# A two-stream transformer kernel on one core: three durations and the pace in its emission clock are changed

## The chip, the cores and the metric

One Trainium2 chip, of which the kernel uses one core. The metric is the device time of one execution, in microseconds (us): the median of several runs. The core has TensorE (PE; its weight loads are shown apart, as PEld), VectorE (DVE), ScalarE (ACT), GpSimd (POOL) and SyncE (SP), which issues the loads from DRAM.

## What is computed

Two blocks, one after the other, on 256 tokens of 1024 features, batch 1. The first block has four layers: short convolution, a state-space mixer (SSM), RWKV-7, short convolution; each is followed by a gated projection and a layer norm. Its output is the x of the second block, which has two layers and a second stream, the context (256 more positions, `ctx`), that doesn't depend on the first block at all before the attention:

```python
def reference(x, ..., c_2, ctx_2, c_ctx_2, ...):
    x = first_block(x, p, conv_w_in, ..., ln_g, ln_b)
    return second_block(x, c_2, ctx_2, c_ctx_2, ...)

def _rwkv_step(state, inp):            # 256 steps, 16 heads of 64
    r_t, w_t, k_t, v_t, kk_t, a_t = inp
    sa = jnp.einsum("bhvk,bhk->bhv", state, -kk_t)
    state = (state * w_t[:, :, None, :] + sa[..., None] * (kk_t * a_t)[:, :, None, :]
             + v_t[..., None] * k_t[:, :, None, :])
    return state, jnp.einsum("bhvk,bhk->bhv", state, r_t)

def second_block(x, c, ctx, ...):
    for l in range(2):
        mod_x = split(silu(c) @ ada_w[l] + ada_b[l])       # the modulation, 9 parts; mod_c alike
        x   = half_ffn(x, ...);   ctx = half_ffn(ctx, ...)     # swiglu, 2816 wide
        y_x, y_c = mixer_ab(hx, hc, ...) if l == 0 else mixer_cd(hx, hc, ...)
        x = half_ffn(x + mod_x[5] * y_x, ...)
        if l == 0: ctx = half_ffn(ctx + mod_c[5] * y_c, ...)
    return x
```

Mixer AB is two sorts of attention whose queries and keys are rms-normed head by head (and rotated, for the tokens); mixer CD is a gated linear recurrence beside a neighbourhood attention.

## The kernel before

Activations lie feature-major: 128 features on the partitions, 256 tokens in the free dimension. A weight is loaded from DRAM as fp32 blocks of 128 x 1024 (`Net.get`, queue SP) and split into two fp32r parts, `whi` by an ACT copy (L599) and `wlo` by a DVE subtraction (L600); a product of it is three fp32r products of 256 columns per chunk of 128 features (`mm3`: hi x hi, hi x lo, lo x hi). The work within the mixers (RWKV heads, SSM, attention) is in fp32 products, of 64, 128 or 256 columns.

Each engine executes its instructions in the order in which it was given them. That order comes from the emission. A generator (`Stream`) emits the instructions of one stream: X is the first block and then the tokens of the second, C is the context. `weave` runs from a clock, `Net.now() = cost + idle`: `cost` is the sum of the durations that `TensorE.matmul` puts on products, `idle` the time in which it believes that TensorE has to wait. Each generator yields where TensorE needs what other engines must first deliver, and is `ready` again at a time that a model of ACT and DVE gives (`Engine.place`: a fixed part and the free size by a rate, in the first gap that is long enough). The first stream in the list that is ready goes on, so C's products fall where the clock sees X waiting. `par` does the same within a stream among two or three chains, such as the heads of RWKV (`heads`, three at a time) or the rms norms of AB (`key` and `head_tile`, two at a time); in the heads, other streams' products go in pieces of 4 chunks, 12 products (`mm3g`, `PIECE`). The third stream, the modulation (`ada`), is emitted by pace: one block each `GAPS` us of the clock, by stage.

During the heads (L1153 and after), C is in its first feed-forward network, whose first half's products are `ps_mm<-h_hi,whi`, `ps_mm<-h_lo,whi` and `ps_mm<-h_hi,wlo`. The recurrence of a pair of heads in chunks of 64 steps goes on in the banks `ps_ca`, `ps_cb` and `ps_mm` with `sv`, `rw_a` and `rw_b`; between its steps ACT and DVE copy from the banks.

`rsqrt` (L677) takes Ln and Exp of the same tile (`tc`) by ACT, then a Newton step by DVE. `act` keeps note of the ACT table set it believes to be there, and issues a load of the set that holds both functions (L393) when Ln comes and the note says another; loads of line 402 are put in when the program is built, ahead of an activation whose function isn't in the set that is there.

A second listing of the names: `x`, `ctx` residual streams; `tc`, `ta`, `tb`, `td` temporaries; `ps_*` PSUM banks; `cs_*` constants; `qb`, `kb` queries and keys of AB.

Of the kernel before, what the change touches and what calls it, by code (L numbers as in the profile page):

```python
# [19 lines left out]
S = 256  # L20
NCH = D // 128
ALPHA = 8 ** 0.25
# [3 lines left out]
# order of emission  # L26
EARLY = 40  # how far back work that nothing waits for may fill an engine's gaps
FINE = 3  # products in pieces in the SSM core (1) and the RWKV heads (2)
PIECE = 4  # K chunks in such a piece
PARTS = 3  # parts of layer 0's modulation that come first  # L30
GAPS = (6.5, 10., 12., 12.)  # the modulation's pace
SLACK = 2  # how far behind VectorE may be for the modulation to go on ...
LATE = 60  # ... unless it is this late
# [3 lines left out]
# ---------------------------------------------------------------- host layout  # L37
def tiles_of(w, cols):
    """[K, M] -> the K x 128 column tiles starting at each entry of cols, as [n, K, 128]."""
    return np.stack([w[:, c:c + 128] for c in cols])  # L40


def blocks(tl, mt=1):
    """[n, K, 128] column tiles -> [n / mt, 128, K / 128 * mt * 128] blocks, K-chunk major."""
# [10 lines left out]
def wsplit(w):  # L55
    """Blocks of 256 columns by half of the K chunks: [M / 256 * 2, 128, 4 * 256]"""
# [5 lines left out]
def fcols(v):  # L62
    """[..., F] -> [128, prod(...) * F / 128]: a feature's value on its partition."""
    v = np.asarray(v)
    return v.reshape(-1, v.shape[-1] // 128, 128).transpose(2, 0, 1).reshape(128, -1)


def tok(x):
    """[T, F] -> [128, F / 128, T]"""
# [17 lines left out]
def constants():  # L87
# [10 lines left out]
    # RWKV chunks of 64 steps: rows beta_s | k_s, columns alpha_t | r_t  # L98
# [35 lines left out]
def rope_head(dim):  # L134
    """cos, sin [S, dim] of the axial rotation, and the [dim, dim] matrix M with rotated = u @ M."""
# [20 lines left out]
def pack(inp):  # L156
    """The input arrays in the layouts that the program loads; no arithmetic."""
# [13 lines left out]
    # SSM: partition (e, p), column pair: group 2 * pair + e, state p  # L171
# [16 lines left out]
    # RWKV  # L188
# [12 lines left out]
    # second block  # L201
# [13 lines left out]
    # heads of A: tile j holds heads j and j + 4, which use the two key heads  # L215
# [21 lines left out]
    # relative position bias spread over query and key positions; positions outside the window hold -1e30  # L237
# [8 lines left out]
    # gains, which the program scales  # L246
# [13 lines left out]
# ---------------------------------------------------------------- the program  # L260
# [1686 lines left out]
```

## Time and profile before

| | |
|---|---|
| three runs | 2931.11, 2926.54, 2930.72 us; median 2930.72 |
| profiled execution | span 2931.2 us; its own time is not listed apart from the runs |
| PE, PEld, DVE, ACT busy | 96%, 90%, 73%, 56% of the span |
| DMA | 454.89 MB, mean 155 GB/s |
| mean granted TensorE clock | 0.985 of full speed |

The profile names groups by line, engine and tile. An fp32 product shows as two records, an fp32r product of 256 columns as one. Records of products overlap, since products are pipelined; the time from one to the next is their pitch. In the order of the work, the first block fills the first 1060 us or so (the heads are at 545 to 785 us), then comes the second block's tokens beside what is left of the context (the tokens' AB projection is at 1535 to 1690 us, their AB attention follows).

### The profile page before, as it was taken

The numbers are of one execution on the slowest core, as the hardware profiler recorded it, in microseconds if no ns is written. First come the engines' busy times: TensorE is split into PE (matmuls) and PEld (weight loads), VectorE is DVE, ScalarE is ACT, GpSimd is POOL, SyncE is SP. The second block draws the span as 40 slices with busy tenths as digits, with TensorE's granted clock in tenths as the row PEclk, the third lists the DMA queues.
The fourth block names the chain that finished last, engine by engine and source line by source line (L and its number), as shares of the span: only waits on it lengthen the run. The fifth ranks groups of instructions, "written<-read, shape, count | busy, mean of one in ns | idle before, by whom it ended". The sixth has DMA issues, their size and how long they took to land.

```text
span 2931.2 us, 58792 instructions
## 1 busy us (share of the span) xinstructions
PE 2814.3 (96%) x23798; PEld 2652.5 (90%) x23798; DVE 2142.3 (73%) x4116; ACT 1631.4 (56%) x3069; POOL 16.6 (1%) x42
## 2 busy tenths in 40 slices
PE   8989998899999999999999999999999999999999
PEld 8977788787999999998999978999999999996999
DVE  8876777666678788898898887877855336676655
ACT  5644556766646464778566766544522224466443
POOL 0000000000000000000000000000000000000000
PEclk9989998999999999999999999999999999999999
DMA  7632353200466666666675644666544323221554
GB/s 266 216 130 94 100 185 123 81 23 33 140 213 203 215 201 221 205 194 190 196 224 182 194 155 129 208 223 212 181 144 125 100 82 102 92 87 57 160 182 142
DMA packets 129296, 454.89 MB, mean 155 GB/s; under 512 B 14336, under 2 KB 18688, under 8 KB 128384
## 3 DMA queue, kind: packets, MB, share of 16 engines
q1 hardware_dynamic: 129024, 451.13, 48.3%
q8 instruction: 187, 3.06, 0.4%
q14 instruction: 85, 0.70, 0.1%
HBM read 450.02 MB, written 1.05 MB: 154 GB/s over the span
## 4 chain that ended last, share of the span: by engine, by line
PE 68%; DVE 14%; DMA 8%; ACT 6%; issue 4%; SPq 0%; DVEq 0%; ACTq 0%
PE ps_mm L431 56%; DMA w<-in_ada_dram 7%; PE ps_ca L431 5%; PE ps_cb L431 5%; DVE wlo L600 5%; DVE junk L1354 3%; ACT whi L599 2%; DVE tc L402 1%; PE ps_st L431 1%; PE ps_cb L435 1%; ACT L402 1%; ACT rw_b L402 1%; ACT tc L402 1%; DVE h_lo L402 1%; DMA w<-in_ffn_in_dram 1%
## 5 line engine op out<-in xcount | busy, mean ns | idle before, releaser
L599 ACT ACTIVATE whi<-w 128x1024 fp32r<-128x1024 f32 (+1 forms) x687 | 715.9, 1044 | 731.1 <-PE ps_mm L431 474.1
L600 DVE TENSOR_TENSOR wlo<-w,whi 128x1024 fp32r<-128x1024 f32 (+1 forms) x687 | 826.3, 1204 | 240.7 <-ACT whi L599 238.8
L431 PE MATMUL ps_mm<-h_hi,whi 128*128 128x256 f32 x3024 | 868.0, 289 | 6.1 <-ACT h_hi L402 4.4
L431 PE MATMUL ps_mm<-h_lo,whi 128*128 128x256 f32 x3024 | 856.0, 284 | 2.5 <-DVE h_lo L402 2.4
L431 PE MATMUL ps_mm<-h_hi,wlo 128*128 128x256 f32 x3024 | 853.2, 283 | 3.1 <-DVE wlo L600 3.0
L431 PEld LDWEIGHTS ps_mm<-h_hi,whi 128*128 128x128 f32 x3024 | 569.7, 189 | 15.8 <-ACT h_hi L402 6.3
L431 PEld LDWEIGHTS ps_mm<-h_lo,whi 128*128 128x128 f32 x3024 | 570.2, 189 | 8.7 <-DVE h_lo L402 3.7
L431 PEld LDWEIGHTS ps_mm<-h_hi,wlo 128*128 128x128 f32 x3024 | 570.9, 189 | 7.4 <-DVE wlo L600 4.9
L1354 DVE SCALAR_TENSOR_TENSOR junk<-w,cond 128x1024 bf16<-128x1024 f32 x288 | 351.9, 1222 | 125.9 <-DMA w<-in_ada_dram 124.8
L431 PE MATMUL ps_mm<-d_hi,whi 128*128 128x256 f32 x1232 | 353.4, 287 | 0.9 <-DVE ctx L402 0.4
L431 PE MATMUL ps_mm<-d_hi,wlo 128*128 128x256 f32 x1232 | 348.5, 283 | 3.6 <-DVE wlo L600 3.6
L431 PE MATMUL ps_mm<-d_lo,whi 128*128 128x256 f32 x1232 | 349.6, 284 | 0.0
L431 PEld LDWEIGHTS ps_mm<-d_hi,wlo 128*128 128x128 f32 x1232 | 233.2, 189 | 4.9 <-DVE wlo L600 4.7
L431 PEld LDWEIGHTS ps_mm<-d_hi,whi 128*128 128x128 f32 x1232 | 232.4, 189 | 4.0 <-issue 2.6
L431 PEld LDWEIGHTS ps_mm<-d_lo,whi 128*128 128x128 f32 x1232 | 232.4, 189 | 2.7 <-issue 1.6
L402 DVE TENSOR_TENSOR td<-td,ps_mm 128x256 f32<-128x256 f32 x154 | 64.5, 419 | 82.3 <-PE ps_mm L431 78.8
L402 ACT ACTIVATE d_hi<-td 128x256 fp32r<-128x256 f32 x154 | 63.0, 409 | 79.2 <-DVE td L402 78.4
L402 ACT ACT_TABLE_LOAD x81 | 103.9, 1283 | 2.5 <-PEq L1938 0.7
L431 PE MATMUL ps_mm<-x_hi,whi 128*128 128x256 f32 x256 | 73.6, 287 | 12.4 <-ACT whi L599 12.4
L402 ACT ACTIVATE tc<-tc 128x256 f32<-128x256 f32 x182 | 75.2, 413 | 6.0 <-DVE tc L402 3.1
L402 ACT ACTIVATE td<-ps_mm 128x256 f32<-128x256 f32 x154 | 57.1, 373 | 33.5 <-PE ps_mm L431 33.1
L431 PE MATMUL ps_mm<-xs_hi,whi 128*128 128x256 f32 x256 | 72.7, 284 | 2.7 <-ACT whi L599 1.6
(459 smaller groups left out, 5466.2 us busy)
## 6 DMA issues: line engine op xcount, KB each, us to landing
w<-in_ffn_in_dram SPq DMA_DIRECT2D x268, 512.0 KB, 4.0
w<-in_ada_dram SPq DMA_DIRECT2D x144, 512.0 KB, 4.3
w<-in_ffn_out_dram SPq DMA_DIRECT2D x96, 512.0 KB, 4.1
w<-in_conv_in_dram SPq DMA_DIRECT2D x64, 512.0 KB, 4.5
w<-in_ffn_out_dram SPq DMA_DIRECT2D x48, 384.0 KB, 3.5
w<-in_ab_in_dram SPq DMA_DIRECT2D x34, 512.0 KB, 4.4
w<-in_ple_gate_dram SPq DMA_DIRECT2D x32, 512.0 KB, 4.4
w<-in_conv_out_dram SPq DMA_DIRECT2D x16, 512.0 KB, 4.6
```

Source lines behind the costliest of these rows:

```text
L402: return f(**kw)
L431: self.t.matmul(out, lhsT=lhsT, rhs=rhs, start=start, stop=stop)
L435: self.t.transpose(out, in_, ident)
L599: nc.scalar.activation(out=hi[:, :n], in_=w[:, :n], func=AF.Copy)
L600: nc.vector.tensor_tensor(out=lo[:, :n], in0=w[:, :n], in1=hi[:, :n].bitcast(F32), op=ALU.subtract)
L1354: nc.vector.scalar_tensor_tensor(out=self.junk, in0=w, scalar=1.0, in1=cb[:, s], op0=ALU.mult, op1=ALU.mult, accum_out=m[:, t, s:s + 1])
```

## The change

Four numbers of the emission clock, and what follows from them for the order. An fp32r product is priced 0.011 us longer (256 columns: 0.1087 to 0.1197 us, the constant 0.002 included), an fp32 product with 33 to 64 output rows 0.055 us shorter (64 columns: 0.115 to 0.060 us), a scan on DVE at 1/1.9 of the rate, and the pace of the modulation is stretched from 6.5, 10, 12 and 12 us to 7.2, 11, 13 and 13. No instruction's form or data changes. The rest of the diff takes out comments and docstrings; since the scan's rate adds a line, what stood on L402 and L431 stands on L403 and L432.

```diff
-GAPS = (6.5, 10., 12., 12.)  # the modulation's pace
+GAPS = (7.2, 11., 13., 13.)
...
             ins = [v for k, v in kw.items() if hasattr(v, "tensor") and k not in ("out", "accum_out")]
-            end = self.place(max(m.ready(v, self) for v in ins + outs), self.fixed + free_size(outs[0]) / self.rate)
+            rate = self.rate / 1.9 if name == "tensor_tensor_scan" else self.rate
+            end = self.place(max(m.ready(v, self) for v in ins + outs), self.fixed + free_size(outs[0]) / rate)
...
         if rhs.dtype == F32R:
-            dur = n / 2400.0
+            dur = n / 2400.0 + 0.011
         elif m > 64:
             dur = max(n, 128) / 600.0
         else:
-            dur = 0.06 + max(n, 32) / (1200.0 if m > 32 else 2400.0)
+            dur = 0.005 + max(n, 32) / 1200.0 if m > 32 else 0.06 + max(n, 32) / 2400.0
         self.count(dur + 0.002, out, [lhsT, rhs])
```

As built, the number of PE products is the same; weight blocks loaded and split rise by 4 (blocks that both streams want and that were shared), ACT table loads from 114 to 144.

TensorE in the RWKV heads, where a head (`rw_a_5503`, in bank `ps_cb`) comes to the end of its preparation while the one in `ps_ca` is in its recurrence. `h_hi`, `h_lo` with `whi`, `wlo` are the context's products. Before:

```order
L431 MATMUL ps_cb<-rw_a_5503 128x128 x8
L435 MATMUL ps_cb<-cs_base,rw_a_5503 128x64 x4
L431 MATMUL ps_ca<-sv_4376,rw_b_5501 64x64 x2
L431 MATMUL ps_mm<-rw_b_5507 64x64
L435 MATMUL ps_cb<-cs_base,rw_a_5503 128x64 x4
L431 MATMUL ps_ca<-rw_a_5500,rw_b_5501 64x64 x2
L431 MATMUL ps_cb<-sv_4376,rw_b_5504 64x64 x2
L431 MATMUL ps_mm<-cs_base,rw_b_5507 64x64 x5
L431 MATMUL ps_ca<-sv_4376,rw_b_5501 64x64 x2
L431 MATMUL ps_ca<-rw_b_5501,sv_4376 64x64 x2
L431 MATMUL ps_cb<-rw_a_5503,rw_b_5504 64x64 x2
L431 MATMUL ps_mm<-cs_base,rw_b_5507 64x64 x3
```

And now:

```order
L432 MATMUL ps_cb<-rw_a_5503 128x128 x8
L436 MATMUL ps_cb<-cs_base,rw_a_5503 128x64 x4
L432 MATMUL ps_ca<-sv_4376,rw_b_5501 64x64
L432 MATMUL ps_ca<-rw_a_5500 64x64
L432 MATMUL ps_ca<-sv_4376,rw_b_5501 64x64
L432 MATMUL ps_ca<-rw_a_5500 64x64
L432 MATMUL ps_mm<-h_hi,wlo 128x256
L432 MATMUL ps_mm<-h_hi,whi 128x256
L436 MATMUL ps_cb<-cs_base,rw_a_5503 128x64 x4
L432 MATMUL ps_ca<-rw_a_5500,rw_b_5501 64x64 x2
L432 MATMUL ps_cb<-sv_4376,rw_b_5504 64x64 x2
L432 MATMUL ps_mm<-h_lo,whi 128x256
```

The context's products, of which there was none before among these steps, now stand between the groups of a head's 64-column products.

ScalarE in the tokens' AB projection, where the rms norms of the heads' keys and queries take Ln (`tc<-ps_st,fixed_66`) and Exp with Square (`tc<-tc`) beside the splits of weights (`whi<-w`). Before:

```order
L402 ACTIVATE tc<-ps_st,fixed_66 128x256
L402 ACTIVATE tc<-tc 128x256 x2
L599 ACTIVATE whi<-w 128x1024
L402 ACTIVATE ta<-kb_12361 128x256
L402 ACTIVATE tc<-ps_st,fixed_66 128x256
L402 ACTIVATE tc<-tc 128x256 x2
L402 ACTIVATE ta<-kb_12361 128x256
L599 ACTIVATE whi<-w 128x1024
L402 ACTIVATE tc<-ps_st,fixed_66 128x256
L402 ACTIVATE tc<-tc 128x256 x2
```

And now:

```order
L403 ACT_TABLE_LOAD
L403 ACTIVATE tc<-ps_st,fixed_66 128x256
L600 ACTIVATE whi<-w 128x1024
L403 ACT_TABLE_LOAD
L403 ACTIVATE tc<-tc 128x256
L403 ACTIVATE ta<-kb_12938 128x256
L403 ACTIVATE tc<-tc 128x256
L600 ACTIVATE whi<-w 128x1024 x2
L403 ACT_TABLE_LOAD
L403 ACTIVATE tc<-ps_st,fixed_66 128x256
L403 ACT_TABLE_LOAD
L403 ACTIVATE tc<-tc 128x256 x2
```

Each Ln and each Exp now has a table load ahead of it; before, none stood among them, after one load ahead of the first. Among the 22 loads more in this projection, those of some eight to twelve norms come in such pairs.

## Rows read from the trace of the kernel before

**Rows 1.** The page: span, busy time by engine, shares of the chain that ended last.
```profile
span 2931.2 us, 58792 instructions
...
PE 2814.3 (96%) x23798; PEld 2652.5 (90%) x23798; DVE 2142.3 (73%) x4116; ACT 1631.4 (56%) x3069; POOL 16.6 (1%) x42
...
PE 68%; DVE 14%; DMA 8%; ACT 6%; issue 4%; SPq 0%; DVEq 0%; ACTq 0%
```

**Rows 2.** The chain of waits in order of time: start us, us, what.
```profile
2106.35 339.99 PE ps_mm L431 x2831
```

**Rows 3.** Windows of the heads: stretch, length, busy PE, PEld, DVE, ACT, POOL, clock, DMA share, GB/s.
```profile
545.00:785.00 240.00, 222.86 (x3461) 189.22 (x3462) 148.62 (x362) 160.36 (x424) 0.00 (x0) 0.96 0.16 49
560.00:740.00 180.00, 169.57 (x2933) 143.29 (x2934) 110.24 (x281) 116.35 (x333) 0.00 (x0) 0.98 0.09 30
740.00:780.00 40.00, 40.00 (x433) 35.41 (x430) 20.50 (x37) 26.16 (x56) 0.00 (x0) 1.00 0.43 133
```

**Rows 4.** The same windows, instructions on tile whi alone; no POOL column.
```profile
545.00:785.00 240.00, 52.53 (x260) 40.35 (x260) 19.56 (x16) 17.84 (x17) 0.96 0.16 49
560.00:740.00 180.00, 22.84 (x112) 17.35 (x112) 8.54 (x7) 8.10 (x8) 0.98 0.09 30
740.00:780.00 40.00, 25.66 (x128) 19.85 (x129) 9.80 (x8) 7.78 (x8) 1.00 0.43 133
```

**Rows 5.** The same windows, tile wlo alone; no ACT and POOL columns.
```profile
545.00:785.00 240.00, 37.13 (x129) 24.32 (x130) 19.56 (x16) 0.96 0.16 49
560.00:740.00 180.00, 15.98 (x56) 10.52 (x56) 8.54 (x7) 0.98 0.09 30
740.00:780.00 40.00, 18.22 (x64) 11.99 (x64) 9.80 (x8) 1.00 0.43 133
```

**Rows 6.** Groups by line and form, PE, 545 to 785 us: busy us, mean ns, idle before.
```profile
L431 PE MATMUL ps_st<-rw_b,cs_base 128*128 128x256 f32 x34 | 11.4, 418 | 1.0 <-ACT rw_a L402 0.9
...
L431 PE MATMUL ps_cb<-cs_base,rw_b 128*64 128x64 f32 x192 | 9.9, 227 | 0.0
...
L431 PE MATMUL ps_ca<-rw_a 128*128 128x128 f32 x48 | 6.6, 283 | 0.0
...
L431 PE MATMUL ps_mm<-rw_a 128*128 128x128 f32 x32 | 5.3, 323 | 0.0
...
L431 PE MATMUL ps_mm<-rw_b,cs_base 128*128 128x256 f32 x10 | 3.5, 431 | 0.1
```

**Rows 7.** Timeline of PE in the heads: start us, us, what.
```profile
746.77 0.69 PE L431 MATMUL ps_cb<-cs_base,rw_b 128*64 128x64 f32 x16
```

**Rows 8.** Groups by form, DVE, whole span: the SSM's scan.
```profile
L402 DVE TENSOR_TENSOR_SCAN ssm_s<-rho,ssm_s 128x128 f32<-128x128 f32 x64 | 23.5, 411 | 0.0
```

**Rows 9.** Groups by form, ACT, whole span: table loads.
```profile
L402 ACT ACT_TABLE_LOAD x81 | 103.9, 1283 | 2.5 <-PEq L1938 0.7 <-PE ps_mm L431 0.4
...
L393 ACT ACT_TABLE_LOAD x33 | 42.3, 1283 | 0.6
```

**Rows 10.** Timeline of ACT around one table load.
```profile
1386.46 1.06 ACT L599 ACTIVATE whi<-w 128x1024 fp32r<-128x1024 f32 x1 [1.56 <-issue]
1387.54 1.28 ACT L402 ACT_TABLE_LOAD   x1
1388.83 0.38 ACT L402 ACTIVATE td<-ps_mm 128x256 f32<-128x256 f32 x1
```

**Rows 11.** Windows of AB: projection, two pieces of it, attention; columns as in rows 3.
```profile
1535.00:1690.00 155.00, 148.26 (x1117) 142.01 (x1116) 135.58 (x258) 108.71 (x181) 0.00 (x0) 0.99 0.59 189
...
1640.80:1644.20 3.40, 0.70 (x5) 0.47 (x4) 2.16 (x4) 3.03 (x4) 0.00 (x0) 1.00 0.33 129
1644.20:1647.60 3.40, 3.40 (x18) 3.31 (x17) 3.40 (x8) 0.90 (x1) 0.00 (x0) 0.50 0.45 143
...
1690.00:1830.00 140.00, 138.62 (x956) 110.63 (x956) 111.75 (x238) 90.77 (x166) 0.00 (x0) 1.00 0.45 141
```

**Rows 12.** Waits, 1580 to 1690 us: us in total, times, longest us.
```profile
ACT whi L599 <- PE ps_mm L431: 21.5, 17, 2.8
```

## The prediction

> **What bounds the kernel now.** I read the page first, then the chain of waits, then the stretches one by one. The page puts TensorE at 96% busy and gives PE 68% of the chain that ended last [rows 1]. The chain shows what sort of work this is: one piece of it runs 339.99 us through 2831 products with nothing ahead of it [rows 2]. That is 339.99 / 2831 = 0.120 us for one fp32r product of 256 columns. So an fp32r product that is moved gains 0.120 us if it lands where TensorE would stand idle, and nothing if it lands where TensorE is full. Hence I look for stretches in which TensorE is not full and in which the change alters what stands on its queue. Two matter: the RWKV heads (545 to 785 us) and the tokens' AB projection (1535 to 1690 us).
>
> **How full TensorE is in the heads.** Its busy row says 222.86 of 240 us [rows 3], but matmul records overlap, so I count by pitch. Two pieces of evidence set it. Sixteen records of 64 columns took 0.69 us [rows 7], and one lasts 0.227 us [rows 6]: (0.69 - 0.227) / 15 = 0.031 us from one to the next. Wider fp32 records last 0.283 us (128 columns) and 0.418 us (256) [rows 6]; with the same overlap their pitches are 0.031 + 0.056 = 0.087 and 0.031 + 0.191 = 0.222 us. The context's products here are the 260 on whi and 129 on wlo [rows 4, 5]: 389 x 0.120 = 46.7 us. The other 3461 - 389 = 3072 records [rows 3] are the heads' own: 78 of 256 columns (four groups, of 34, 20, 14 and 10) and 128 of 128 columns (three, of 48, 48 and 32; the first and the last of each stand in [rows 6]) make 17.3 + 11.1 us, the other 2866 x 0.031 make 88.8 us, in all 117.2 (0.038 each on average). Work: 163.9 of 240 us; 76 us, **32%, is lost** to the chain that runs from TensorE to VectorE or ScalarE and back. From 560 to 740 us, where the context has 112 + 56 = 168 products, the same count gives 20.2 + 2765 x 0.038 = 125.3 of 180, 30% lost. From 740 to 780, with 128 + 64 = 192 context products in 40 us, it is 23.0 + 241 x 0.038 = 32.2, 19.5% lost [rows 3 to 5]. More context work, less loss.
>
> **The change, part by part.** No product is added or taken away; the prices only steer the emission.
>
> 1. *Heads.* With 64-column products at 0.06 us and not 0.115 us, the clock no longer credits the heads' products with time that they don't take, and it sees TensorE waiting. By the order, context products among the heads' products go from 480 to 936, and they now stand between the steps of a head's recurrence, where before runs of over 400 products held none. The 456 more (456 x 0.120 = 54.7 us) leave a later place where the context ran densely, at the chain's pitch. The heads' stretch then holds 163.9 + 54.7 = 218.6 us of work. At the loss of 740 to 780 us, the nearest stretch with much context work, it lasts 218.6 / 0.805 = 271.6, 31.6 more; the net is 54.7 - 31.6 = **-23 us**. The bounds: all of it in gaps that exist (-54.7), or a loss that stays at 30% (218.6 / 0.70 = 312, +72, net +18). The value taken is that of the row that is most like what the order shows.
>  With the 19 weight blocks (24 products each) come 19 loads of 512 KB on SP's queue, issued earlier, 19 splits on ScalarE (17.84 / 17 = 1.05 us) and VectorE (19.56 / 16 = 1.22 us) [rows 4], and, by the order, 11 more table loads of 1.283 us [rows 9]: ScalarE 160 + 20 + 14 = 194 and VectorE 149 + 23 = 172 of some 270 us [rows 3]. The DMA share there is 0.16, and 0.43 where the context is dense [rows 3]. I cost all these at nothing: idle time covers them. If that cover fails, the loss nears 30%, which is the upper bound above.
>
> 2. *Tokens' AB projection.* In before, eight rsqrts run behind one table load, because Ln and Exp follow each other in ScalarE's order; now each of them has a load ahead of Ln and another ahead of Exp. By the order 22 loads more: 22 x 1.283 = 28.2 us of ScalarE [rows 9]. ScalarE idles 155 - 108.7 = 46 us in this stretch [rows 11], and 21.5 us of the wait of its weight splits is for TensorE, to free a buffer [rows 12]: slack that a load may use. But an rsqrt gets 2.57 us longer, the rotation's product stands in TensorE's queue behind it, and what fills the time in between is some 37 products, 4.4 us by the order. Bounds 0 and 28.2; ScalarE's slack covers the sum but not each chain, so I take a bit under half: **+12 us**.
>  A timeline of ScalarE shows such a load start 0.02 us after the activation ahead of it ended, and the activation behind it 0.01 us after the load [rows 10]: the load costs its 1.28 us and no more. The Trainium skill ("ScalarE: Activation LUTs", section "What ACT_TABLE_LOAD costs") adds a drain of about 1380 ns to every switch, 2.66 us in all; by it the 22 loads would be 58.5 us of ScalarE, an estimate from that page, more than the idle time there, and the sum would turn to no gain. The trace does not agree, and the measurement decides.
>
> 3. *Tokens' attention.* 101 context products fewer stand in it, used up ahead of it: 0 to 12.1 us (101 x 0.120). The AB core as it is shows TensorE busy 138.62 of 140 us [rows 11], so little waits there: **+3 us**.
>
> 4. *At nothing:* scans at 1/1.9 of the rate (a 128-wide one lasts 411 ns [rows 8]; the clock had 70 + 128 / 0.96 = 203 and now has 323; it moves a few ssm products; bounds 4 us either way, since the SSM's first part has no second stream to fill from); the new GAPS (6.5 / 0.1087 = 59.8 products of clock before, 7.2 / 0.1197 = 60.2 now: the pace in products stays); four more weight blocks loaded twice for the CD part (4 x 1.05 us on ScalarE, under what it idles there).
>
> Sum: -23 + 12 + 3 = **-8 us**. The profiled execution spans 2931.2 us [rows 1]; its own time isn't listed, and the span is 0.5 us above the median of the three runs (2926.54, 2930.72, 2931.11), so what lies around it is too small to matter here. From the median: 2930.72 - 8 = **2922 us**. A change of 0.2%, 5.9 us, is about what a measurement of this kernel can tell from none.
>
> **The rivals.**
>
> - *The gaps take nearly all.* The weight-load row is 189.22 of 240 us in the heads against 222.86 for the products [rows 3]. If TensorE is really free where it loads no weights, 50.8 us, then 50.8 of the 54.7 us fit: -51 + 12 + 3 = -36, **2895 us**. For it: my own count by pitch has more free time still (76 us). Against: the free time lies behind single waits, and a run of 12 context products (1.4 us) delays the recurrence that it stands ahead of. The Trainium skill ("Perfetto Trace Analysis", section "Identifying the Most-Contended Engine") calls matmul busy time no measure of TensorE's headroom and takes the weight loads' busy share in its place; by that rule this rival is right.
> - *It moves work and gains nothing.* The busy row taken at its word: 240 - 222.86 = 17.1 us free [rows 3], so -17 + 12 + 3 = -2, **2929 us**. The same comes if the chip's recurrence waits on other steps than the clock's, so that the change doesn't do what it says: the order is new and the waits stay.
> - *Table loads become the bound, slower.* In the tokens' AB projection every chain waits for its own two loads: +28.2. A split of a weight is queued behind them, TensorE stalls for 3 us, and its clock falls: after such a stall (0.70 us busy of 3.40) it ran 3.40 us at 0.50 of full speed, the lower of its two levels, 1.2 GHz [rows 11], 1.7 us lost each time; eight rsqrts, 13.6 us. -23 + 28.2 + 13.6 + 3 = +22, **2953 us**. It decides once more than 20 us of the loads and their stalls show. For it: TensorE waits on ScalarE and VectorE there already. Against: the 21.5 us of slack [rows 12].
> - *Fill in the wrong places, slower.* The heads' loss stays at 26%, half-way from 19.5 to 32: 218.6 / 0.74 = 295, which gives back the whole 54.7; with 12 + 3 and nothing to set against them, +15, **2946 us**. It decides above 22%, where the 39.7 us that the other terms leave are used up (218.6 / 0.78 = 280). For it: pieces of three to twelve context products now stand directly ahead of 64-column products that are on the chain. Against: 740 to 780 us, where such a mix lost 19.5%.
>
> **How the numbers follow.** The forecast (2914 to 2930 with the heads' loss from 17 to 22%) has 0.36, of which 0.26 is faster than 2924.9 and 0.10 within 0.2%; the fuller gain 0.20, faster; no gain 0.14, the same; the table loads 0.17 and the wrong places 0.13, slower. Faster 0.26 + 0.20 = 0.46, the same 0.10 + 0.14 = 0.24, slower 0.17 + 0.13 = 0.30. Cases of both signs hold the chance, so: the likeliest alone is 2914 to 2930; the range for 8 in 10 is 2892 to 2952, from the fuller gain to the loads, and leaves out what lies beyond: 2876 with all 54.7 us gained and nothing lost, 2964 with the heads' loss at 30% and the other terms kept.
>
> **What would show it.** Right: the heads' stretch some 30 us longer with about 840 context products (389 + 456), and weight-load busy per us above 0.79; the context's dense run after the heads some 55 us shorter; table loads 114 to 144 in the whole; TensorE's idle time in the tokens' AB projection up by about 12 us, behind ScalarE. Wrong: a heads' stretch longer by over 50 us (wrong places) or by under 10 (the fuller gain); an AB projection longer by 25 us or more with pieces at a clock of 0.50 (the loads), or not longer at all; a difference that arises elsewhere, above all in the SSM or the CD part, which I hold for unchanged.

## The result, and the profile after

The change makes the kernel slower: 2975.86 us median (2973.14 to 2979.87, 4 runs) against 2930.91 (2926.54 to 2934.46, 4 runs); the ratio is 1.0159, 95% interval 1.0144 to 1.0174. That is 45 us; the prediction was 8 us faster, with a range from 2892 to 2952. The profiled execution spans 2973.0 us, 41.8 more than before's [rows 1].

The page of the change:

```profile
span 2973.0 us, 58833 instructions
...
PE 2832.0 (95%) x23798; PEld 2667.8 (90%) x23798; DVE 2149.2 (72%) x4120; ACT 1672.9 (56%) x3103; POOL 16.7 (1%) x42
...
PE 72%; DVE 10%; ACT 8%; DMA 6%; issue 3%; SPq 0%; ACTq 0%; DVEq 0%
```

TensorE does the same 23798 records in 17.7 us more of busy time. ScalarE's share of the chain that ended last rises from 6% to 8%, VectorE's and the DMA's fall. The page alone names no culprit: ScalarE is busy 56% as before. So the two stretches that the prediction rests on are compared, each from the same product to the same product. First before: the heads, from the first product on `rw_a` in bank `ps_ca` to the last of `sv,rw_b` in `ps_cb`, and the tokens' AB projection, from the first to the last rotation (`ps_ca<-tb,second`). The columns are those of [rows 3].

```profile
548.00:777.00 229.00, 214.16 (x3393) 181.50 (x3394) 140.44 (x346) 152.60 (x408) 0.00 (x0) 0.96 0.14 44
1544.00:1689.00 145.00, 138.27 (x1036) 132.33 (x1037) 125.61 (x238) 101.89 (x168) 0.00 (x0) 0.99 0.59 185
```

The same two stretches of the change:

```profile
548.00:825.00 277.00, 263.78 (x3820) 228.65 (x3821) 170.04 (x383) 189.23 (x449) 0.00 (x0) 0.98 0.23 71
1556.00:1717.00 161.00, 143.45 (x1035) 135.92 (x1035) 127.77 (x240) 130.43 (x191) 0.00 (x0) 0.96 0.51 164
```

The heads take 48 us more for 427 more records; the AB projection does the same records as before in 16 us more, with ScalarE 28.5 us busier. Its table loads that were put in when the program was built (groups by form, ScalarE, the AB stretch of the change); with the 7 of line 393 that makes 39, where before had 8 and 7, 15 in all:

```profile
L403 ACT ACT_TABLE_LOAD x32 | 41.1, 1283 | 0.6
```

To see where all of the 41.8 us came from, I count TensorE's work by pitch, as the prediction did: 0.120 us for an fp32r product, 0.031 for a 64-column record. For fp32 records of 128 and 256 columns I take 0.109 and 0.215 and not the prediction's 0.087 and 0.222 (in before, 15 records of 128 columns on `ps_mm<-p,kl` take 1.84 us and one lasts 0.275, which gives 0.112; four of 256 columns on `ps_ca<-kava,qa` take 1.03 us and one lasts 0.391, which gives 0.213). I take this work from the time between two products that both kernels have. What is left is lost time, in us; the last three columns are runs of the next section:

| stretch | before | change | change, loads cured (e3) | 64-column price, cured (e8) | e15 |
|---|---|---|---|---|---|
| up to the heads | 88.8 | 86.5 | 85.4 | 86.2 | 84.3 |
| heads | 69.5 | 67.6 | 55.7 | 54.8 | 50.4 |
| rest of the first block | 15.9 | 18.9 | 20.0 | 13.9 | 7.7 |
| from there to the tokens' AB projection (the context's AB) | 20.1 | 33.6 | 34.8 | 20.0 | 27.5 |
| tokens' AB projection | 11.6 | 28.1 | 11.7 | 4.6 | 5.6 |
| tokens' attention | -5.2 | 0.9 | 1.9 | -7.2 | -7.6 |
| up to the CD mixer | 13.8 | 20.8 | 21.1 | 21.7 | 26.9 |
| from there on | 16.5 | 16.2 | 16.2 | 16.5 | 13.5 |
| sum | 231.0 | 272.6 | 246.8 | 210.5 | 208.3 |

(A negative value means that the pitches are a little too high for that mixture; the differences between columns are what counts. The sums differ as the spans do: 41.6 here, 41.8 there.) The heads lost no less than before although 49 us of work had been moved into them; the AB projection lost 16.5 us more, and another 23.5 us were lost in places that the prediction held for nearly unchanged: 3.0 in the rest of the first block, 13.5 at the context's AB, 7.0 after the attention.

Some of this is TensorE's clock. The mean granted clock of the profiled execution is 0.980 of full speed, and it was 0.985 before: (1 - 0.980) x 2973.0 = 59 us of full clock that weren't granted, for (1 - 0.985) x 2931.2 = 44. So up to 15 of the 41.8 us were lost at the lower clock; it is an upper bound, since TensorE waits for part of that time, too. The clock falls behind stalls, as [rows 11] and an instance below show, so this is a second price of stalls rather than a cause of its own.

### The profile page after: what moved, and what is told of

It reads as the page before. It is cut to its first block, busy times and chain, and to the rows that moved or that the text cites. A ratio compares the mean times of both kernels' runs of the same rounds, so it can differ in the third digit from the quotient of the medians.

```text
span 2973.0 us, 58833 instructions
## 1 busy us (share of the span) xinstructions
PE 2832.0 (95%) x23798; PEld 2667.8 (90%) x23798; DVE 2149.2 (72%) x4120; ACT 1672.9 (56%) x3103; POOL 16.7 (1%) x42
## 3 DMA queue, kind: packets, MB, share of 16 engines
HBM read 452.12 MB, written 1.05 MB: 152 GB/s over the span
## 4 chain that ended last, share of the span: by engine, by line
PE 72%; DVE 10%; ACT 8%; DMA 6%; issue 3%; SPq 0%; ACTq 0%; DVEq 0%
PE ps_mm L432 59%; PE ps_ca L432 5%; PE ps_cb L432 5%; DMA w<-in_ada_dram 4%; DVE wlo L601 3%; DVE junk L1355 2%; ACT whi L600 2%; ACT L403 2%; PE ps_st L432 1%; DVE tc L403 1%; ACT tc L403 1%; PE ps_cb L436 1%; DMA w<-in_ffn_in_dram 1%; DMA w<-in_ab_in_dram 1%; DVE r L403 1%
## 5 line engine op out<-in xcount | busy, mean ns | idle before, releaser
L432 PE MATMUL ps_mm<-h_hi,whi 128*128 128x256 f32 x3024 | 871.0, 289 | 14.8 <-ACT h_hi L403 8.6
L432 PE MATMUL ps_mm<-h_hi,wlo 128*128 128x256 f32 x3024 | 859.6, 285 | 1.6 <-DVE wlo L601 1.5
L432 PE MATMUL ps_mm<-h_lo,whi 128*128 128x256 f32 x3024 | 859.4, 285 | 1.6 <-DVE h_lo L403 1.5
L432 PEld LDWEIGHTS ps_mm<-h_hi,whi 128*128 128x128 f32 x3024 | 574.3, 190 | 26.9 <-ACT h_hi L403 10.8
L432 PEld LDWEIGHTS ps_mm<-h_lo,whi 128*128 128x128 f32 x3024 | 572.9, 190 | 7.1 <-DVE h_lo L403 2.8
L432 PEld LDWEIGHTS ps_mm<-h_hi,wlo 128*128 128x128 f32 x3024 | 571.9, 189 | 4.8 <-DVE wlo L601 2.8
L432 PE MATMUL ps_mm<-d_hi,whi 128*128 128x256 f32 x1232 | 356.3, 290 | 4.2 <-ACT whi L600 3.3
L432 PE MATMUL ps_mm<-d_hi,wlo 128*128 128x256 f32 x1232 | 349.8, 284 | 4.3 <-DVE wlo L601 4.3
L432 PE MATMUL ps_mm<-d_lo,whi 128*128 128x256 f32 x1232 | 351.9, 286 | 0.4 <-DVE d_lo L403 0.4
L432 PEld LDWEIGHTS ps_mm<-d_hi,whi 128*128 128x128 f32 x1232 | 235.1, 191 | 10.0 <-ACT whi L600 3.7
L432 PEld LDWEIGHTS ps_mm<-d_hi,wlo 128*128 128x128 f32 x1232 | 234.5, 191 | 5.3 <-DVE wlo L601 4.7
L432 PEld LDWEIGHTS ps_mm<-d_lo,whi 128*128 128x128 f32 x1232 | 234.0, 190 | 3.8 <-issue 1.8
L403 ACT ACT_TABLE_LOAD x106 | 136.0, 1283 | 3.3 <-PEq L1939 0.7
L403 DVE TENSOR_TENSOR td<-td,ps_mm 128x256 f32<-128x256 f32 x154 | 64.2, 417 | 93.6 <-PE ps_mm L432 90.8
L403 ACT ACTIVATE d_hi<-td 128x256 fp32r<-128x256 f32 x154 | 62.9, 409 | 87.9 <-DVE td L403 87.5
L432 PE MATMUL ps_mm<-x_hi,whi 128*128 128x256 f32 x256 | 73.6, 288 | 11.5 <-ACT whi L600 11.5
L403 ACT ACTIVATE tc<-tc 128x256 f32<-128x256 f32 x182 | 75.2, 413 | 3.0 <-DVE tc L403 0.4
L403 ACT ACTIVATE td<-ps_mm 128x256 f32<-128x256 f32 x154 | 57.3, 373 | 34.5 <-PE ps_mm L432 33.4
L432 PE MATMUL ps_mm<-xs_hi,whi 128*128 128x256 f32 x256 | 72.8, 284 | 3.2 <-DVE tb L403 3.2
```

The costliest lines, as they stand in the source:

```text
L403: return f(**kw)
L432: self.t.matmul(out, lhsT=lhsT, rhs=rhs, start=start, stop=stop)
```

## Experiments

### One price at a time, and the table loads cured

e1 is before with one line of the change, e2 the change with that line taken back:

```diff
# e1, against before
-            dur = 0.06 + max(n, 32) / (1200.0 if m > 32 else 2400.0)
+            dur = 0.005 + max(n, 32) / 1200.0 if m > 32 else 0.06 + max(n, 32) / 2400.0
# e2, against the change
-            dur = 0.005 + max(n, 32) / 1200.0 if m > 32 else 0.06 + max(n, 32) / 2400.0
+            dur = 0.06 + max(n, 32) / (1200.0 if m > 32 else 2400.0)
```

**e1**, expected: 

> The change's price of 64-column products alone (0.060 for 0.115 us); the fp32r price, the scans' rate and the pace stay as before. By the order: 696 context products among the heads' (341 in before, 749 in the change, counted from the first rw_a product to the last sv,rw_b one), 30 table loads in the tokens' AB projection (24 in before, 46 in the change). Theory P (the heads gain nothing from the fill, and the work that was moved there is missed later): heads stretch about 228.6 + 355 x 0.116 = 270 us, the time up by 20 to 28 us to some 2955. Theory L (the loss is the table loads of the tokens' AB projection and what they stall): heads the same 270, but the time within 6 us of before, 2925 to 2937.

**e2**, expected: 

> The change without its price of 64-column products: fp32r price, scans and pace as changed. By the order 315 context products among the heads', 47 table loads in the tokens' AB projection. Theory P: the AB projection loses some 16 us more than before and nothing else does, about 2947. Theory L: nearly all of the change's 45 us, 2965 to 2976.

Measured: e1 2928.65 us, ratio 0.9998 (0.9988 to 1.0009), no difference; e2 2977.12 us, 1.0162 (1.0145 to 1.0180), the whole loss. The price of 64-column products, the one that moves the 400 products into the heads, is not what costs. Of theory P the first half holds, for the heads of e1 lose 67.0 us with 25 table loads, hardly less than before's 69.5; but the moved work isn't missed later, so the theory doesn't explain the 45 us.

e3 is the change with a cure of the table loads. The note in `act` goes wrong where a Silu that was emitted ahead of the load of the common set (L393) is carried out between that load and its Ln: the load is pinned behind the instruction emitted just ahead of it, the Silu isn't. The note then says "ln" while neither set is there, no common load is issued again, and each Ln and each Exp gets its own. In the change's order on ScalarE, the last common load is the second row of line 393, and its Ln is the row with `ps_mm`, behind the Silu (`td<-ps_mm`):

```
L393 ACT_TABLE_LOAD
L403 ACTIVATE tc<-ps_st,fixed_66 128x256
L393 ACT_TABLE_LOAD
L403 ACTIVATE tc<-tc 128x256
L403 ACT_TABLE_LOAD
L403 ACTIVATE td<-ps_mm 128x256
L403 ACTIVATE tc<-tc 128x256
L403 ACT_TABLE_LOAD
L403 ACTIVATE tc<-ps_mm,fixed_66 128x256
```

The cure holds the load behind the last activation of another set, too:

```diff
-            self.tc.keep_in_program_order(self.A.preload_act_table_set("natural_log_exp_and_others"))
+            i = self.tc.keep_in_program_order(self.A.preload_act_table_set("natural_log_exp_and_others"))
+            if self.other is not None:
+                self.tc.add_manual_dep(i.ins, self.other.ins.name, mybir.DependencyInfo(mybir.DependencyClass.NoSync, mybir.DependencyReason.DATA), reason="table")
...
-        return self.A.activation(out=out, in_=in_, func=func, **kw)
+        i = self.A.activation(out=out, in_=in_, func=func, **kw)
+        if func not in (AF.Ln, AF.Exp, AF.Copy, AF.Square):
+            self.other = i
+        return i
```

**e3**, expected: 

> The change with each load of the set that holds Ln and Exp held behind the last activation of another set, so that no Silu can come between the load and its Ln; the emission is the same. By the order 113 table loads (144 in the change), 29 of them in the tokens' AB projection (46). Theory P: the AB projection's 16 us come back, the rest stays, about 2958. Theory L: most of the 45 us come back, 2940 or less. If the loads had been hidden: 2972 or more.

Measured: 2947.55 us, ratio 1.0060 (1.0041 to 1.0079): 28 of the 45 us come back, between the two expectations. The same two stretches of e3:

```profile
548.00:812.00 264.00, 257.34 (x3808) 224.37 (x3809) 165.55 (x371) 176.53 (x434) 0.00 (x0) 0.99 0.23 75
1545.00:1690.00 145.00, 137.65 (x1036) 132.17 (x1036) 127.90 (x241) 108.87 (x174) 0.00 (x0) 0.99 0.57 182
```

The AB projection is back at before's 145 us. How a load gets onto the path shows in the waits there; the change first (us in total, times, longest), then e3:

```profile
DVE tc L403 <- ACT tc L403: 18.2, 11, 3.5
...
PE ps_ca L432 <- DVE tb L403: 10.2, 8, 3.3
```

```profile
PE ps_ca L432 <- DVE tb L403: 3.6, 5, 1.1
...
DVE tc L403 <- ACT tc L403: 1.9, 4, 0.7
```

And one instance in the timeline of the change: a load, the Exp, a weight's split, the Square; VectorE's steps wait for them, and the rotation on TensorE for VectorE, 3.33 us. In the 4 us from 1609 TensorE then runs at 0.50 of its clock (last row, a window):

```profile
1602.85 1.28 ACT L403 ACT_TABLE_LOAD   x1
...
1604.14 0.42 ACT L403 ACTIVATE tc<-tc 128x256 f32<-128x256 f32 x1
1604.47 1.04 ACT L600 ACTIVATE whi<-w 128x1024 fp32r<-128x1024 f32 x1
...
1605.41 0.40 ACT L403 ACTIVATE tc<-tc 128x256 f32<-128x256 f32 x1
...
1605.85 0.42 DVE L403 SCALAR_TENSOR_TENSOR tc<-ps_mm,tc 128x256 f32<-128x256 f32 x1 [0.97 <-ACT tc L403]
...
1607.71 1.22 PE L432 MATMUL ps_ca<-tb,second 128*128 128x256 f32 x2 [3.33 <-DVE tb L403]
...
1609.00:1613.00 4.00, 2.76 (x13) 2.47 (x13) 2.95 (x6) 1.67 (x3) 0.00 (x0) 0.50 0.00 0
```

The heads gain by the cure as well, 12 us, with 8 loads fewer there (21 for 29 in the traces). How a load gets onto their path shows in one place. In the change, ScalarE makes a norm's Ln at 648.25 us and a copy that the heads need (`rw_b<-ps_ca`) at 655.64, 7.4 us later, with three table loads in between (649.01, 651.58 and 653.72). In e3 no load stands between the same two, and the copy comes after 4.2 us (643.11 and 647.32). The last of the three loads, and TensorE's wait for that copy (total, times, longest), which e3 hasn't; in all, TensorE's listed waits in the heads are 14.2 us in the change and 6.2 in e3:

```profile
653.72 1.28 ACT L403 ACT_TABLE_LOAD   x1
...
PE ps_ca L432 <- ACT rw_b L403: 3.8, 1, 3.8
```

e4 is the change in which only X is asked while the heads are emitted (`streams[:1] if self.fine else streams` in `weave`).

**e4**, expected: 

> The change, but the context emits nothing while the heads do; by the order 72 context products stay in the stretch (emitted ahead of it), 677 fewer. If a fill product in the heads costs its own pitch (theory P: no free room was used), the heads last about 276 - 677 x 0.116 = 198 us and the time stays near the change's, 2965 to 2985. If the fill did use free room, the heads stay over 215 us and the time goes up by the 17 us or more that were hidden, to 2990 or more.

Measured: 3011.24 us, ratio 1.0284 (1.0262 to 1.0307). The heads last 194.9 us, 81.2 less than in the change, just the pitch of the 677 products (81.2): what the first theory says. But the whole takes 35 us longer. In the profiled executions, 32.5 us apart, 17 more are lost in the rest of the first block, 13 of them right behind the heads, where the next products then have no cover, 8 in the AB projection, 5 ahead of the heads. Its heads have 10 loads for 29, too, so the price of a fill product and that of its loads can't be parted in this run. Inconclusive for the heads; it says that the fill as a whole is worth having.

### The other prices alone

**e5**, before with `dur = n / 2400.0 + 0.011` for fp32r, expected: 

> The change's fp32r price alone (0.1197 for 0.1087 us for 256 columns); the pace stays 6.5, 10, 12, 12, so that the modulation's blocks come with fewer products between them. By the order 336 context products among the heads', 46 table loads in the tokens' AB projection (24 in before). If those loads are what the change's other half costs: 16 us in the AB projection and no more, about 2947. If the fp32r price also moves the context's work so that the attention of both streams loses (16 us remained in the run with the loads cured): about 2963.

**e6**, before with the new `GAPS`, expected: 

> The change's pace alone (7.2, 11, 13, 13). By the order 341 context products among the heads' as in before, 40 table loads in the tokens' AB projection. If the loads are the whole of it: 16.5 x 16 / 22 = 12 us, 2942. If the pace itself costs (a modulation that comes later is awaited): more, 2950 or over.

**e7**, before with `self.rate / 1.9` for scans, expected: 

> The change's scan rate alone. By the order 324 context products among the heads', 32 table loads there (23 in before), 24 in the tokens' AB projection as in before. If a table load among the heads costs its time on the chain, as the run with the loads cured says (8 loads fewer, 12 us less lost): 9 more cost 10 to 13 us, 2940 to 2944. If ScalarE's idle time covers them: 2927 to 2933.

**e8**, e1 with the cure of e3, expected: 

> The price of 64-column products alone, and the loads cured. By the order 112 table loads (129 without the cure, 114 in before), 16 of them among the heads (30), 30 in the AB projection (30). If a load among the heads costs 1.1 to 1.5 us: 14 x 1.1 = 15 us or more under the run with that price alone, 2908 to 2914, faster than before. If not: 2925 to 2930.

Measured: e5 2986.43 us, 1.0184 (1.0167 to 1.0202), more than either expectation: the fp32r price alone does worse than the whole change. e6 2952.56 us, 1.0073 (1.0058 to 1.0088), in the range of the upper expectation (the pace itself costs), though 18 of its 20 us are lost in the AB projection, where the trace has 33 loads. So the fp32r price and the pace each bring such loads by themselves (40 in e5); the 64-column price hardly does (18 in e1, 15 in before). e7 2930.76 us, 0.9996 (0.9985 to 1.0006): no difference, but as a sum: the heads lost 7.9 us more, with 27 loads for 18, and the SSM ahead of them 8.8 us less. e8 2913.50 us, 0.9944 (0.9928 to 0.9960): faster than before, as expected; the heads lost 12.2 us less than in e1, with 14 loads for 25. So a load among the heads is worth about 1 us on the chain (12.2 / 11, 7.9 / 9, and 11.9 / 8 in e3): most of its 1.283 us was not covered. In e8 and e3 the emission is that of the run beside it and the loads alone differ; in e7 the order differs, too.

### Why the fp32r price costs without the loads

Cured, the change is still 34 us behind e8 (2947.55 against 2913.50). My theory at this point: the clock holds VectorE's and ScalarE's steps for too short (256 columns 0.337 and 0.313 us; in the trace 0.42 to 0.48 and 0.37 to 0.50), so it lets a chain's next product come too soon. The old fp32r price, a tenth too low, made up for that, because each product that was put in between covered more than it was charged for. If so, raising the engines' times takes the loss away, and only together with the new price. The edit:

```diff
-        self.V, self.A = Engine(self, nc.vector, 0.07, 960.0, 0.25), Engine(self, nc.scalar, 0.1, 1200.0, 0.15)
+        self.V, self.A = Engine(self, nc.vector, 0.15, 960.0, 0.25), Engine(self, nc.scalar, 0.18, 1200.0, 0.15)
```

**e9**, e8 with the scans' rate, expected: 

> The change with its fp32r price and its pace set back to those of before, and the loads cured: the 64-column price and the scans' rate alone. By the order 696 context products among the heads', 118 table loads, 30 in the AB projection. If the 34 us between the two cured runs so far (2947.55 and 2913.50) come from the fp32r price and the pace: 2908 to 2920. If from the scans' rate beside the 64-column price: 2935 or more.

**e10**, e6 with the cure, expected: 

> The pace alone (7.2, 11, 13, 13), and the loads cured. By the order 107 table loads (132 without the cure), 27 in the AB projection (40). The pace alone cost 21 us, 18 of them in the AB projection. If the loads were all of it: 2925 to 2932, and less by up to 8 if the heads' 7 loads fewer pay there too. If the pace itself costs: 2940 or more.

**e11**, e3 with the engines' times, expected: 

> The change with the loads cured, and VectorE's and ScalarE's fixed parts in the clock set near the traced ones as well (0.15 and 0.18 us for 0.07 and 0.10: 0.417 and 0.393 us for 256 columns, traced 0.42 and 0.37 to 0.41). By the order 880 context products among the heads' (749). If the fp32r price does harm because the clock then lets too few products stand between the steps of a chain whose VectorE and ScalarE times it holds too short (the old price, 0.011 us too low, made up for it): most of the 34 us come back, 2912 to 2930. If not: 2940 or more.

**e12**, e8 with the engines' times, expected: 

> The price of 64-column products alone, the loads cured, and the two engines' fixed parts as in the run before this. By the order 820 context products among the heads' (696), 114 table loads. If the engines' times are what the emission lacks: under the 2913.5 of the run without them, 2895 to 2910. If the fp32r price of before already makes up for them: 2908 to 2925, no better.

**e13**, before with the cure, expected: 

> The kernel before with the loads cured and nothing else. By the order 102 table loads (114), 16 among the heads (23), 24 in the AB projection (24). At the 1.1 us that a load fewer among the heads was worth in two pairs of runs: 8 us faster, 2919 to 2925. If the cure is worth nothing where the AB projection has no pairs of loads: 2927 to 2932.

**e14**, the change without the scans' rate, cured, expected: 

> The change without its scan rate, and the loads cured: the 64-column price, the fp32r price and the pace. By the order 708 context products among the heads', 114 table loads, 27 in the AB projection. If the fp32r price with its pace is what the cured change still loses (34 us against the 64-column price alone): 2940 to 2948. If the scans' rate is: 2913 to 2925.

**e15**, e14 with the engines' times, expected: 

> The run before this one with the two engines' fixed parts at 0.15 and 0.18 us. By the order 875 context products among the heads', 113 table loads. If the fp32r price does harm for want of those times: 20 us or more under the run before this one, and 2905 to 2918 in all. If it was chance that the cured change came back to 2914 with them: no clear difference.

**e17**, e5 with the cure, expected: 

> The fp32r price alone, loads cured, on the old price of 64-column products, the old pace and the old scans. By the order 336 context products among the heads', 113 table loads, 29 in the AB projection. The uncured run of it cost 55 us, with 25 loads more than before in the AB projection. If the fp32r price costs by itself (theory: it takes away what made up for too short times of VectorE and ScalarE): 2940 or more, against 2922.72 of the kernel before with the cure. If the loads were all of the 55 us: 2919 to 2928.

**e18**, e17 with the engines' times, expected: 

> The run before this one with the two engines' fixed parts at 0.15 and 0.18 us. By the order 381 context products among the heads', 115 table loads, 28 in the AB projection. If the want of those times is the reason: 15 us or more under the run before this one. If the 48 us between the two runs with the 64-column price were the luck of those two orders: any sign, or within 10 us.

Measured, all cured (medians, and the ratio to the kernel before, which has no cure):

| | engines' times as before | near the traced ones |
|---|---|---|
| 64-column price (e8, e12) | 2913.50, 0.9944 | 2931.96, 1.0023 |
| with fp32r price and pace (e14, e15) | 2959.58, 1.0104 | 2911.81, 0.9937 |
| with the scans' rate too (e3, e11) | 2947.55, 1.0060 | 2914.12, 0.9956 |
| fp32r price alone (e17, e18) | 2967.25, 1.0124 | 2938.36, 1.0032 |
| none of the prices (e13) | 2922.72, 0.9973 | |

The intervals of the ratios reach 0.0009 to 0.0026 to either side. Three runs missed their expectations: e9 (2927.76) fell between its two, e12 and e14 came out above both of theirs.

With the old times of the engines the fp32r price costs 46 us (e14 less e8, with the pace) and 44.5 us (e17 less e13); beside the scans' rate, as in the change itself, it is 20 (e3 less e9, with the pace). Setting those times nearer the traced ones gives back 48, 33 and 29 us in the three rows that have the price, and costs 18 us where it is missing. The pace is nothing by itself (e10 2922.81 against e13 2922.72; its 20 us in e6 were the loads). The scans' rate costs 14 us beside the 64-column price (e9 2927.76 against e8), with 15.6 us more lost in the heads and 5 loads more there, and gains 12 in e3 against e14: its sign depends on the rest.

By the count of lost time, the price costs most in the tokens' AB projection (13.4 us in e14 less e8, 14.0 in e17 less e13), in the rest of the first block (9.6, 7.0) and at the context's AB (5.5, 7.2). The engines' times give the first two back (12.4 and 15.7 in e15, 18.1 and 10.1 in e18), but nothing at the context's AB nor up to the CD mixer, where e15 loses 2.0 and 4.2 us more and e18 11.3 and 9.8. The clock has its part: the mean granted clock is 0.978 in e17 for 0.985 in e13, and 0.981 in e14 for 0.986 in e8, which is up to 21 and 15 us of full clock; e15 has 0.988.

What the want of products may look like, in waits at the end of the first block, where TensorE takes the residual `r`; e14, then e15:

```profile
PE ps_mm L432 <- DVE r L403: 4.3, 1, 4.3
```

```profile
PE ps_mm L432 <- DVE r L403: 1.4, 1, 1.4
```

And in the tokens' AB projection of e14, one wait of 10 us for the last rotation, which e15 hasn't (5.6 us lost there in all, for 18.0); below it, a row of VectorE within it:

```profile
PE ps_ca L432 <- DVE tb L403: 12.0, 6, 10.0
...
1689.89 1.23 DVE L1360 SCALAR_TENSOR_TENSOR junk<-w,cond 128x1024 bf16<-128x1024 f32 x1 [2.12 <-DMA w<-in_ada_dram]
```

This wait (1684.53 to 1694.53 us) isn't a want of products alone. ScalarE makes two table loads in it (1684.61 and 1686.31), for a Silu that stands between a Ln and its Exp, which the cure doesn't prevent; and the steps that the rotation needs stand on VectorE behind steps of the modulation, one of which waited 2.12 us for its weight.

The interaction was seen on three orders (two of them differ by the scans' rate alone), so it is hardly the luck of one; a few us of each number are, since single stalls of 5 to 10 us come and go with an order. What the runs show is that the fp32r price and the engines' times belong together. That the price acts through too thin a cover is argued from it and not shown, and the engines' times without any new price were not run.

### The splits in the heads

e16 is e3 with both splits of a weight on GpSimd (`nc.gpsimd.tensor_copy`, `nc.gpsimd.tensor_tensor`) while the heads are emitted.

**e16**, expected: 

> The change with the loads cured, and the splits of the weights that come during the heads done by GpSimd, which idles there, and not by ScalarE and VectorE; the emission is the same. By the order 749 context products among the heads'. If the heads' remaining loss (55.7 us in the cured change) comes from splits that stand ahead of a head's copies on ScalarE and VectorE: 45 us or less there, 2937 or less in all. If it comes from the products that stand ahead of a head's on TensorE: 53 to 60 us, and the time within 6 us of 2947.55; later, if GpSimd is too slow for the weights.

Measured: 2990.76 us, 1.0207 (1.0190 to 1.0224); the heads lost 82.8 us for 55.7. It doesn't answer the question, since the splits are slow there (GpSimd's copies take 1084 ns each, its subtractions more than twice that) and VectorE's own work gets longer beside them. GpSimd's subtractions in e16 (whole span), then one group of VectorE's (heads) in e16 and in e3:

```profile
L607 POOL TENSOR_TENSOR wlo<-w,whi 128x1024 fp32r<-128x1024 f32 x35 | 85.2, 2436 | 2.6
```

```profile
L403 DVE SCALAR_TENSOR_TENSOR tc<-tc 128x256 f32<-128x256 f32 x15 | 10.6, 708 | 0.1
```

```profile
L403 DVE SCALAR_TENSOR_TENSOR tc<-tc 128x256 f32<-128x256 f32 x14 | 5.8, 417 | 0.1
```

Whether splits or TensorE's own queue hold the heads' remaining 55 us stays open.

## Why the prediction was wrong

- **Heads, "-23 us": came to -2.** The count of the moved work was near (750 context products for 341, 49 us by pitch, where 54.7 were forecast), and so was the rate once the loads are out of the way: e3 loses 55.7 of 263.5 us there, 21%, where 19.5% was taken, and gains 14 us. But the change's stretch grew by 48 us for those 49, where 31.6 were forecast. The step that failed is "I cost all these at nothing: idle time covers them". ScalarE did idle a third of the stretch, but table loads stand ahead of copies that the heads wait for, as in the instance above. The 11 loads more (29 for 18 in the traces) took nearly all that the fill gave: with 8 of the 29 gone, e3 gets 12 us back. What the splits did there stays open (e16). I had read their cover from ScalarE's share of the stretch, not from who waits behind them. The weight-load rows still show 277 - 228.65 = 48 us free in the change's heads; the Trainium skill ("Perfetto Trace Analysis", section "Identifying the Most-Contended Engine") judges TensorE's headroom by that share, beside the rate that the products reach; by it the rival of the fuller gain would have been right. The trace agrees only in part: e3, e8 and e15 lose 14, 15 and 19 us less than before in the heads, and no run fills the 48. Headroom isn't the same as a place in the order where a product fits.
- **Tokens' AB projection, "+12 us": 16.5.** The mechanism was right, the size short: 24 loads more, and the cure takes back 16.4. The load again takes 1283 ns with no gap behind it: in the timeline of the change the Exp starts at 1604.14, 0.01 us after it. (The Trainium skill, "ScalarE: Activation LUTs", section "What ACT_TABLE_LOAD costs", would have 2.66 us a switch, 64 us for 24 loads, an estimate; no run here shows that.) The low clock behind a stall came as the rival of the table loads said, but smaller: the stretch had 0.96 for 0.99, so 161 x 0.04 - 145 x 0.01 = 5 us of full clock, not 13.6, and 16.5 us is far from its 28.2 + 13.6.
- **Tokens' attention, "+3 us": 6.1** (-5.2 to 0.9), within its bounds of 0 and 12.1, but by luck. The reason given was that the heads use the products up ahead of it; e1 and e8, which move them into the heads, lose no more there than before (-7.8 and -7.2), and e2 and e5, which don't move them, lose 1.0 and 0.8. The pace alone has it too (e6, 0.1). So it comes with the fp32r price or the pace.
- **What was missing: the fp32r price itself.** The prediction priced where products were moved in the heads and the attention, and held the scans, the pace and four more weight blocks at nothing; what the new order of the fp32r products costs elsewhere has no term in it. 23.5 us of the 41.6 lie in three such places (rest of the first block, context's AB, after the attention). The price by itself costs 44.5 us (e17 less e13), 20 in the change's own setting (e3 less e9, with the pace), beside the 28 of the loads; with the engines' times nearer the traced ones the loss is gone in the sum beside the 64-column price (e11, e15), but 16 us are left without it (e18 less e13). Place by place it is not all shown: the first two of the three grow with the price, but after the attention e8, which hasn't the price, loses 21.7 us, and e15 26.9, for 13.8 before; that stays open. I had read the new number as a correction (0.1197 against 0.120 in the chain) and not asked what else in the clock the old one made up for.
- **At nothing, as said:** the pace (e10 against e13). The scans too, in sum (e7), but by luck: +7.9 us in the heads against -8.8 ahead of them, each twice the bound of 4 that was set.
- **A reading.** The pitch of 0.087 us for 128-column records was too low (0.112 in the run of records above), 3 us of work in the heads; it changes no term.
- **The rivals.** The table loads were the cause of most of the loss, 28 of 45 us, and got 0.17; that rival had them in the AB projection alone, where the cure takes back 16.4. The sums of its case (2953) and of the wrong places (2946) each lack the fp32r term. The upper end of 2952 would have had to hold several of them at once.

By the runs: cure alone -7 us (e13), 64-column price with the cure -17 (e8), all of the change but the scans with the cure and the engines' times -19 (e15, 2911.81 us, ratio 0.9937, interval 0.9922 to 0.9952). e15, e8 and e11 beat both kernels clearly; by their intervals these three can't be ranked.

## What to carry to other kernels

Prices in a clock that sets an order work as a set: a wrong one may be what makes up for another, as the fp32r price and the engines' times did here, so set the two sides of a race (here TensorE's products, and the VectorE and ScalarE steps that they have to cover) right together, and try the pair as well as each alone. An engine that idles a third of a stretch doesn't cover an extra instruction that stands ahead of a chain's own: ask who waits behind it. And where a new order changes the number of table loads, count them by stretch before anything else: 28 of 45 us came back by pinning one kind of instruction.

## What the runs showed of the hardware that I had not expected

VectorE's work took longer while GpSimd was busy beside it: the same 128x256 operation 708 ns on average in e16's heads, 417 in e3's. Only some operations are hit: of those 15, the 11 that met none of GpSimd's took 406 to 426 ns, one that met one for a third of its length 426, and the three that lay mostly beside one took 1147, 1942 and 2535. All groups that were hit in those heads work from SBUF to SBUF, and none that reads a PSUM bank was hit: of the 12 `td<-td,ps_mm` of the same size, the nine that lay beside GpSimd's work took 405 to 423 ns, no longer than the other three. A 128x1024 subtraction took GpSimd 2436 ns, twice VectorE's 1.22 us [rows 4], while its cast of that size took 1084 ns, about ScalarE's 1.05 us [rows 4].
